# Turned probabilities in the weights' raw buffers, a tick between rotation and split, and earlier loads of queries and keys

## The chip, the cores and the metric

The kernel runs on one core of a Trainium2 chip. The core has a matrix engine (TensorE, PE in the profile, with its weight loads as PEld), a vector engine (VectorE, DVE), a scalar engine (ScalarE, ACT), a general engine (GpSimd, POOL) and a queue engine (SyncE, SP) that here only issues DMAs. The engines run side by side, each in the order of its own instructions, and wait for each other by semaphores. The metric is the device time of one execution in microseconds (us).

## What is computed

Two layers (DEPTH = 2) over 512 positions of width 2048. One projection of the layer's input is cut into three groups of heads, each 128 wide; every group is gated, all are joined, projected back, added to the input and normalised.

```python
    fq, fk, fv, fg, f_logit, dq, dk, dv, dg, iq, ik, iw, mq, mg = jnp.split(h, offsets, axis=-1)
    y_fox = fox_attention(heads(fq, H_FOX), ..., cum_logf) * silu(fg)           # 6 heads, causal, log-forget bias
    y_dsa = dsa_attention(rope(dq), rope(dk), dv, q_idx, k_idx, w_idx) * silu(dg) # 6 heads, rotated, top-128 keys
    y_mem = memory_attention(mq, k_mem, v_mem) * silu(mg)                        # 4 heads on 256 memory rows
    y = jnp.einsum('bsn,nd->bsd', jnp.concatenate([y_fox, y_dsa, y_mem], axis=-1), w_out)
    x = layer_norm(ALPHA * x + y, ln_gain, ln_bias)
```

The sparse heads (`d`) pick 128 keys per query by an index score; in the kernel that choice is a mask which is added to the scores. The forgetting heads (`f`) add a bias that falls with distance. Everything is float32.

## The kernel before

**Precision and tiling.** Each float32 operand is split in two float32r parts: ScalarE copies the high part, VectorE subtracts to get the low part (`split`, lines 216 to 218). A product is three matmuls, high x high, high x low, low x high (`product`, lines 224 to 226). Weights come in chunks of 128 x 2048; a chunk is two halves of 128 x 1024, and the main loop does one half per step: step n = 2i + h is half h of chunk i.

**Stages of a layer.** Memory keys and values, an index stage, the value stage (`vs` chunks: seven products in place of eight, for all columns that are handled in blocks), the heads stage (eight chunks `fq`, `fk`, `dq`, `dk` of heads 4 and 5, with the attention of eleven heads and one memory head between their matmuls), and the output stage (`out` chunks). A step takes 24 matmuls of 512 columns in the heads stage and 12 in the value and output stages.

**Weights.** `load_w(i + 2)` at the first step of chunk i issues both halves of chunk i + 2 on SyncE's queue (line 263), into two of the seven raw buffers of the pool `raws` (4 KB per partition each). `split_w(n + 3)` in step n splits half n + 3 into one of four pairs of `whl`. A raw buffer is free again when VectorE has made the low part. Some chunks are no loads at all: they are grown from a raw buffer that is kept (`grow_w`, `make_w`); of some others (`pair`) both halves of two blocks are loaded and added.

**Everything else** lies in 69 slots of 128 x 512 (2 KB per partition), among them the 32 of the layer's input, which stay. A slot or a raw buffer that the program asks for is one whose last use lies earlier in the program's order; the first instruction on it waits for that use to be over. SyncE issues in order, so a load that waits for its slot holds up all loads behind it.

**Order of the head work.** It is written out as generators: each `yield 1` ends a piece, and `tick` runs one piece of each active generator. The heads stage has two ticks per step, one in the middle of the chunk's matmuls and one behind them, 32 in all. `begin(gen, wait)` puts a generator in the list, and it sits out `wait` ticks first.
- `head_turn(l, v)` is called once per step, v = 0 to 15. It loads the queries and keys of the head that `TURNS` has at v + 2 (`load_qk`, two loads by line 998), begins `qk_head` of the head at v + 1, and begins `attend` of the head at v.
- `qk_head` turns the queries by PE transposes (line 1005), rotates them if the head is a sparse one (`rope`, lines 589 to 592: four VectorE operations, one of full height by the cosines, two of half height by the sines, one sum), splits them, ends its piece, and does the same for the keys.
- `attend` has five pieces: scores, masked minimum (line 763), exponentials (line 767), and the load of the gates; the load of the values; ten transposes of the probabilities in three PSUM tiles (line 788) and their split; the gates (`tanh`, line 507) and the split of the values; the product with the values (`po`) and the multiplication by the gates. The probabilities are divided by their sums (lines 771 and 774) at the next break in the chunk's matmuls.
- The turned probabilities are two tiles of 512 columns and one of 256: slots `pth` and `ptl` for each of the first two, one slot `pthl` for both parts of the third. They live from the third piece to the fifth.

`PRODUCTS` order, `OUT_ORDER` and the sums of weights that GpSimd's queue makes in DRAM (line 417) run beside all this and are paced by the ticks.

Of the kernel before, what the change touches and what calls it, by code (L numbers as in the profile page):

```python
# [11 lines left out]
F32 = mybir.dt.float32  # L12
F32R = mybir.dt.float32r
# [4 lines left out]
P = 128  # L18
DM = 2048
# [30 lines left out]
EARLY = 4  # L50
# [33 lines left out]
PAIRS = 6  # L84
# [92 lines left out]
def kernel(  # L177
# [13 lines left out]
    nc = tc.nc  # L191
# [11 lines left out]
    def uid(name):  # L203
        count[0] += 1
        return f"{name}_{count[0]}"

    def slot(name, dt=F32, w=512):
        return slots.tile([P, w], dt, tag="s", name=uid(name))
# [20 lines left out]
    chunks = stream()  # L229
# [14 lines left out]
    H = DM // 2  # L244

    def half(src, h):
        return src[:, h * H:(h + 1) * H]

    def load_w(i, pieces=2):
        if i < len(chunks) and chunks[i][4][0] != "grown":  # L250
            kind, key = chunks[i][4]
            src = {"wall": lambda: wall[key], "sum": lambda: sums[key],
                   "pair": lambda: wall[key[0]]}[kind]()
            if chunks[i][0] == "out" and chunks[i][2][0] == "Q6":
                raw[i] = [[slot("grown") for _ in range(2)] for _ in range(2)]
                for c in range(4):
                    nc.sync.dma_start(raw[i][c // 2][c % 2], src[:, c * 512:(c + 1) * 512])
                return
            raw[i], w = [], DM // pieces
            for c in range(pieces):  # L260
                if c * 2 % pieces == 0:
                    raw[i].append(raws.tile([P, H], F32, tag="raw", name=uid("raw")))
                nc.sync.dma_start(raw[i][-1][:, c * w % H:c * w % H + w], src[:, c * w:(c + 1) * w])
                if i < 3 and c * 2 % pieces == 0:
                    load_mem(2 * i + c * 2 // pieces)
                if kind == "pair":
                    for e in (2 * c, 2 * c + 1):
                        t = slot("other")
                        nc.sync.dma_start(t, wall[key[1]][:, e * 512:(e + 1) * 512])
                        others[i, e] = t  # L270
# [207 lines left out]
    def begin(gen, wait=0, last=False, whole=False, but=None):  # L478


        active.append([wait, gen, last, whole, but])
# [105 lines left out]
    def rope(ps, cos, sin, pairs, rows, name):  # L587
        t1, t2 = slot(name), slot(name)
        nc.vector.tensor_tensor(t1[:rows], ps[:rows], cos[:rows], op=ALU.mult)
        for a, b, n in pairs:  # L590
            nc.vector.tensor_tensor(t2[a:a + n], ps[b:b + n], sin[b:b + n], op=ALU.mult)  # L591
        nc.vector.tensor_tensor(t1[:rows], t1[:rows], t2[:rows], op=ALU.add)
        return t1
# [150 lines left out]
    def attend(l, kind, h):  # L744
        key = (kind, h)
        if kind == "f":
            bt = pr = biases.pop(h)
        q, k = qs.pop(key), ks.pop(key)
        ps = [bank("s") for _ in range(3)]
        for qb in (3, 1, 0, 2):  # L750
            b, off, w = PACK[qb]
            product(ps[b][:, off:off + w], tuple(a[:, qb * P:(qb + 1) * P] for a in q),
                    tuple(a[:, :w] for a in k), True, True)
        if kind == "d":
            assert l in chosen
            bt = masks[l]
            pr = [slot("pr", w=w) for w in BANK_W]
        nm, sums, rec = small("nm", 4), small("sums", 4), small("rec", 4)

        for qb in (3, 1, 0, 2):  # L760
            b, off, w = PACK[qb]
            c = slice(off, off + w)
            nc.vector.tensor_tensor_reduce(pr[b][:, c], ps[b][:, c], bt[b][:, c], -SCALE, -TAKEN,  # L763
                                           ALU.add, ALU.min, nm[:, qb:qb + 1])
        for qb in (3, 1, 0, 2):
            b, off, w = PACK[qb]
            nc.scalar.activation(pr[b][:, off:off + w], pr[b][:, off:off + w], AF.Exp,
                                 bias=nm[:, qb:qb + 1], scale=-1.0, accum_out=sums[:, qb:qb + 1])

        def probabilities():  # L770
            nc.vector.reciprocal(rec, sums)
            for qb in (3, 1, 0, 2):
                b, off, w = PACK[qb]
                nc.scalar.activation(pr[b][:, off:off + w], pr[b][:, off:off + w], AF.Copy,
                                     scale=rec[:, qb:qb + 1])

        before.append(probabilities)
        n = HEADS.index(key)
        load_head(("g", key), GATES + n // 4, n % 4)
        yield 1  # L780
        load_head(("v", key), VALUES + n // 4, n % 4)
        yield 1
        tp = [bank("pt") for _ in range(3)]
        for kt in range(4):
            tb, toff = PT_PACK[kt]
            for qb in range(kt, 4):
                b, off, w = PACK[qb]
                nc.tensor.transpose(tp[tb][:, toff + (qb - kt) * P:toff + (qb - kt + 1) * P],
                                    pr[b][:, off + kt * P:off + (kt + 1) * P], ident)
        pt = []  # L790
        for b in range(3):
            w = PT_W[b]
            if w == 512:
                hi, lo = slot("pth", F32R), slot("ptl", F32R)
            else:
                both = slot("pthl", F32R)
                hi, lo = both[:, :w], both[:, w:]
            split(tp[b][:, :w], hi, lo)
            pt.append((hi, lo))
        yield 1  # L800
        gate(key, turned(("g", key), "gt"))
        v = slot("vh", F32R), slot("vl", F32R)
        split(vraw.pop(("v", key)), *v)
        yield 1
        po = bank("po")
        for kt in range(4):
            tb, toff = PT_PACK[kt]
            w = SEQ - kt * P
            product(po[:, kt * P:], tuple(a[:, kt * P:(kt + 1) * P] for a in v),
                    tuple(a[:, toff:toff + w] for a in pt[tb]), kt == 0, kt == 3)  # L810
        heads_out(head_number(key), key, po)
# [196 lines left out]
    def load_qk(key):  # L1008
        for e in range(2):
            load_head(("qk"[e], key), (FOXQ if key[0] == "f" else DSAQ) + e, key[1])  # L1010

    def qk_head(key):
        for name, to in (("q", qs), ("k", ks)):
            t = turned((name, key), "qk")
            if key[0] == "d":
                t = rope(t, cos_d, sin_d, HALVES, P, "rope")
            hi, lo = slot("qh", F32R), slot("ql", F32R)
            split(t, hi, lo)
            to[key] = (hi, lo)
            yield 1  # L1020

    def head_turn(l, v):

        if v + 2 in TURNS and TURNS[v + 2][1] < EARLY:
            load_qk(TURNS[v + 2])
        if v + 1 in TURNS and TURNS[v + 1][1] < EARLY:
            key = TURNS[v + 1]
            begin(qk_head(key), 1)
            if key[0] == "f":
                load_ck(l, key[1])  # L1030
                begin(forget_bias(l, key[1]), 1)
        if v in TURNS:
            begin(attend(l, *TURNS[v]), 1 + (v in (11, 15)), whole=True)
        if v in MEM_TURNS:
            begin(mem_head(l, MEM_TURNS[v]), whole=True)
        if v in (8, 10, 12, 14):
            first_difference(v // 2 - 4)
        if v == 14:
            begin(early_operands())
# [159 lines left out]
    for i, (kind, l, j, col, _) in enumerate(chunks):  # L1199
# [28 lines left out]
        for h in range(2):  # L1228
            n = 2 * i + h
            grow_w(n + 2)  # L1230
            if h == 0 and i > 0:
                load_w(i + 2)
                if 2 <= i < 6:
                    for k in range(4 * i - 8, 4 * i - 4):
                        load_xt(k)
                elif i == 7:
                    load_tables()
# [134 lines left out]
            begin(top_keys(l), whole=True)  # L1372
        if kind == "vs" and (name, pair, col) == ("Q6", 0, 1) and l > 0:
            begin(residual_rows(l), whole=True)
        if kind == "vs" and (name, col) == ("Q3", 1):
            if pair in (1, 3, 5):
                begin(mem_head(l, pair // 2), whole=True)
            if pair == PAIRS - 3:
                load_ck(l, 0)
                load_qk(("f", 0))  # L1380
            elif pair == PAIRS - 2:
                begin(qk_head(("f", 0)), 5)
                begin(forget_bias(l, 0), 2)
            elif pair == PAIRS - 1:
                load_ck(l, 4)
                load_qk(("f", 1))
                begin(attend(l, "f", 0), 1, whole=True)
        if kind == "vs" and (name, pair, col) == ("Q3", PAIRS - 1, 1):
            chains.clear()
# [104 lines left out]
```

## Time and profile before

| what | us |
|---|---|
| median of three runs (1976.32 to 1979.19) | 1978.86 |
| the profiled execution, its own time | 1978.29 |
| its span | 1976.5 |
| heads stage of layer 0, by PE's timeline | about 615 to 820 |
| heads stage of layer 1 | about 1600 to 1803 |
| DMA, share of the 16 engines in layer 0's heads stage | 0.91 |

A window's row holds its length, the busy time of each engine with its number of instructions in brackets, the clock that TensorE was granted (1.00 is full), the mean share of the 16 DMA engines, and GB/s. A row of waits holds who waited, by engine, tile and line, behind the arrow what ended the wait, then the total in us, how often, and the longest. SPq is SyncE's queue; a row of its timeline has start, duration until the last of the group was issued, and the number of DMAs.

### The profile page before, as it was taken

To read this page: it belongs to the slowest core of one execution; us is meant where nothing else is said; L and a number is where in the kernel's file an instruction comes from. 1 tells how busy PE (TensorE), PEld (TensorE's weight loads), DVE (VectorE), ACT (ScalarE), POOL (GpSimd) and SP (SyncE) were. 2 spreads that over 40 slices of the span, in tenths; PEclk is the share of its full clock that TensorE was granted. 3 is DMA by queue.
4 is the path that set the end of the run, shared out by engine and by line. 5 is a ranking of instruction groups with operands and counts; after the bars stand their busy time and mean duration, and the time that the engine had idled before them with its cause. 6 is when DMAs were issued, how large, how long until landed. Compare 5 with 4: busy or idle time off the path is not lost.

```text
span 1976.5 us, 26877 instructions
## 1 busy us (share of the span) xinstructions
PE 1904.0 (96%) x9218; PEld 1611.5 (82%) x9218; DVE 1538.6 (78%) x2478; ACT 1061.0 (54%) x1674; POOL 408.6 (21%) x650
## 2 busy tenths in 40 slices
PE   9999999999999889899999999999999998788997
PEld 8998888888888777787899988888888886677876
DVE  6889777889666666888897898888886657578798
ACT  5775444445456654654476754444455565556553
POOL 0122112111113122131062211111211221211311
PEclk9999999999999999999999999999999999999999
DMA  9888889989999989899889867777899998886975
GB/s 352 291 235 224 255 242 274 276 246 279 314 321 300 267 223 263 286 290 310 263 259 280 233 202 203 234 225 214 229 305 313 333 282 244 236 229 207 269 215 140
DMA packets 190004, 511.95 MB, mean 259 GB/s; under 512 B 18656, under 2 KB 71904, under 8 KB 182124
## 3 DMA queue, kind: packets, MB, share of 16 engines
q1 hardware_dynamic: 146508, 303.63, 44.8%
q0 software_dynamic: 43360, 206.62, 42.0%
q8 instruction: 72, 1.18, 0.2%
q14 instruction: 64, 0.52, 0.1%
HBM read 456.67 MB, written 164.65 MB: 314 GB/s over the span
## 4 chain that ended last, share of the span: by engine, by line
PE 78%; DVE 8%; DMA 7%; ACT 4%; issue 2%; SPq 0%; POOL 0%; DVEq 0%; ACTq 0%; POOLq 0%
PE v L226 16%; PE v L224 16%; PE v L225 16%; PE c L226 5%; PE c L224 5%; PE c L225 5%; DMA raw<-in_wall_dram 4%; PE z L225 3%; PE z L226 3%; PE z L224 3%; DMA grown<-in_wall_dram 2%; DVE rope L591 1%; DVE wlo L218 1%; PE ix L704 1%; PE ix L705 1%
## 5 line engine op out<-in xcount | busy, mean ns | idle before, releaser
L218 DVE TENSOR_TENSOR wlo<-raw,whi 128x1024 fp32r<-128x1024 f32 (+1 forms) x513 | 628.4, 1231 | 244.1 <-ACT whi L217 238.6
L217 ACT ACTIVATE whi<-raw 128x1024 fp32r<-128x1024 f32 (+1 forms) x513 | 540.0, 1057 | 461.1 <-PE v L226 310.7
L224 PE MATMUL v<-whi,vxh 128*128 128x512 f32 x768 | 300.3, 391 | 1.0 <-ACT vraw L979 1.0
L226 PE MATMUL v<-whi,vxl 128*128 128x512 f32 x768 | 299.1, 389 | 0.0
L225 PE MATMUL v<-wlo,vxh 128*128 128x512 f32 x768 | 298.9, 389 | 0.0
L224 PE MATMUL v<-whi,xh 128*128 128x512 f32 x576 | 224.2, 389 | 0.0
L226 PE MATMUL v<-whi,xl 128*128 128x512 f32 x576 | 224.1, 389 | 0.0
L225 PE MATMUL v<-wlo,xh 128*128 128x512 f32 x576 | 224.1, 389 | 0.0
L224 PE MATMUL c<-xh,whi 128*128 128x512 f32 (+1 forms) x544 | 203.7, 374 | 0.2 <-DVE nm L763 0.2
L226 PE MATMUL c<-xh,wlo 128*128 128x512 f32 (+1 forms) x544 | 200.2, 368 | 0.0
L225 PE MATMUL c<-xl,whi 128*128 128x512 f32 (+1 forms) x544 | 199.6, 367 | 0.0
L225 PE MATMUL z<-wlo,yh 128*128 128x512 f32 (+1 forms) x434 | 168.8, 389 | 4.2 <-DVE wlo L218 4.2
L224 PEld LDWEIGHTS v<-whi,vxh 128*128 128x128 f32 x768 | 144.2, 188 | 31.4 <-ACT vraw L979 1.8
L226 PEld LDWEIGHTS v<-whi,vxl 128*128 128x128 f32 x768 | 144.2, 188 | 30.1
L224 PE MATMUL z<-whi,yh 128*128 128x512 f32 (+1 forms) x434 | 168.4, 388 | 0.0
L225 PEld LDWEIGHTS v<-wlo,vxh 128*128 128x128 f32 x768 | 144.2, 188 | 29.7 <-DVE wlo L218 0.2
L226 PE MATMUL z<-whi,yl 128*128 128x512 f32 (+1 forms) x434 | 167.8, 387 | 0.0
L225 PEld LDWEIGHTS v<-wlo,xh 128*128 128x128 f32 x576 | 108.1, 188 | 22.7
L224 PEld LDWEIGHTS v<-whi,xh 128*128 128x128 f32 x576 | 108.1, 188 | 22.5
L226 PEld LDWEIGHTS v<-whi,xl 128*128 128x128 f32 x576 | 108.1, 188 | 22.4
L408 POOL TENSOR_TENSOR seen<-mark,mhalf 128x1 f32<-128x1 f32 x87 | 26.7, 307 | 479.0 <-DVE mark L407 449.6
L224 PEld LDWEIGHTS c<-xh,whi 128*128 128x128 f32 x544 | 103.8, 191 | 11.4 <-DVE nm L763 0.7
(232 smaller groups left out, 3449.1 us busy)
## 6 DMA issues: line engine op xcount, KB each, us to landing
raw<-in_wall_dram SPq DMA_DIRECT2D x330, 512.0 KB, 7.2
sum<-in_wall_dram POOLq DMA_DIRECT2D x52, 1024.0 KB, 11.3
raw<-sum SPq DMA_DIRECT2D x88, 512.0 KB, 7.8
v<-vraw POOLq DMA_DIRECT2D x144, 256.0 KB, 6.6
raw<-in_wall_dram POOLq DMA_DIRECT2D x56, 512.0 KB, 7.5
vraw<-v SPq DMA_DIRECT2D x96, 256.0 KB, 7.4
other<-in_wall_dram SPq DMA_DIRECT2D x80, 256.0 KB, 9.1
grown<-sum SPq DMA_DIRECT2D x32, 256.0 KB, 6.5
```

Source lines behind the costliest of these rows:

```text
L217: nc.scalar.activation(hi, src, AF.Copy)
L218: nc.vector.tensor_tensor(lo, src, hi.bitcast(F32), op=ALU.subtract)
L224: nc.tensor.matmul(ps, ah, bh, start=start, stop=False, skip_group_check=more)
L225: nc.tensor.matmul(ps, ah, bl, start=False, stop=False, skip_group_check=more)
L226: nc.tensor.matmul(ps, al, bh, start=False, stop=stop, skip_group_check=more)
L408: nc.gpsimd.tensor_tensor(seen, mark, mhalf, op=ALU.mult)
L591: nc.vector.tensor_tensor(t2[a:a + n], ps[b:b + n], sin[b:b + n], op=ALU.mult)
L704: nc.tensor.matmul(o, st[:, qb * P:(qb + 1) * P], kh2[:, :w], start=True, stop=False)
L705: nc.tensor.matmul(o, st[:, qb * P:(qb + 1) * P], kl2[:, :w], start=False, stop=True)
```

## The change

1. `attend` puts the two tiles of 512 columns in raw buffers, high part in the left half and low part in the right: two raw buffers in place of four slots per head. The third tile stays in its slot.
2. `load_w` can load one half (`some`). For chunks i > 8 whose chunk i + 2 is no `pair`, the first half is loaded at the first step of chunk i and the second half at its second step, in place of both at the first.
3. `qk_head` of a sparse head has three pieces: rotation of the queries; their split, and the rotation of the keys; the split of the keys. A forgetting head's two pieces stay.
4. `attend` of every sparse head in `TURNS` begins with a wait of 2. Before, only those at v = 11 and 15 did, the others with 1.
5. Queries and keys are loaded at v + 3 in place of v + 2, and those of `f` 1 behind product Q5 of the last pair of value columns in place of Q3.

```diff
-    def load_w(i, pieces=2):
+    def load_w(i, pieces=2, some=(0, 1)):
...
-                raw[i] = [[slot("grown") for _ in range(2)] for _ in range(2)]
-                for c in range(4):
-                    nc.sync.dma_start(raw[i][c // 2][c % 2], src[:, c * 512:(c + 1) * 512])
+                for h in some:
+                    t = [slot("grown") for _ in range(2)]
+                    raw.setdefault(i, []).append(t)
+                    for c in range(2):
+                        nc.sync.dma_start(t[c], half(src, h)[:, c * 512:(c + 1) * 512])
...
             for c in range(pieces):
+                if c * 2 // pieces not in some:
+                    continue
...
-            if w == 512:
-                hi, lo = slot("pth", F32R), slot("ptl", F32R)
-            else:
-                both = slot("pthl", F32R)
-                hi, lo = both[:, :w], both[:, w:]
+            both = raws.tile([P, H], F32R, tag="raw", name=uid("pthl")) if w == 512 else slot("pthl", F32R)
+            hi, lo = both[:, :w], both[:, w:]
...
             if key[0] == "d":
                 t = rope(t, cos_d, sin_d, HALVES, P, "rope")
+                yield 1
             hi, lo = slot("qh", F32R), slot("ql", F32R)
             split(t, hi, lo)
             to[key] = (hi, lo)
-            yield 1
+            if key[0] == "f" and name == "q":
+                yield 1
+        yield 1
...
-        if v + 2 in TURNS and TURNS[v + 2][1] < EARLY:
-            load_qk(TURNS[v + 2])
+        if v + 3 in TURNS and TURNS[v + 3][1] < EARLY:
+            load_qk(TURNS[v + 3])
...
-            begin(attend(l, *TURNS[v]), 1 + (v in (11, 15)), whole=True)
+            begin(attend(l, *TURNS[v]), 1 + (TURNS[v][0] == "d"), whole=True)
...
             grow_w(n + 2)
+            if i > 0:
+                late_half = i > 8 and i + 2 < len(chunks) and chunks[i + 2][4][0] != "pair"
+                if late_half:
+                    load_w(i + 2, 2, (h,))
+                elif h == 0:
+                    load_w(i + 2)
             if h == 0 and i > 0:
-                load_w(i + 2)
...
+        if kind == "vs" and (name, pair, col) == ("Q5", PAIRS - 1, 1):
+            load_qk(("f", 1))
...
-                load_qk(("f", 1))
```

More of the change, by code (lines that the diff above doesn't have):

```diff
@@ L254, in load_w @@
             if chunks[i][0] == "out" and chunks[i][2][0] == "Q6":
-                raw[i] = [[slot("grown") for _ in range(2)] for _ in range(2)]
-                for c in range(4):
-                    nc.sync.dma_start(raw[i][c // 2][c % 2], src[:, c * 512:(c + 1) * 512])
+                for h in some:
[3 more added lines that the diff above has]
+                        nc.sync.dma_start(t[c], half(src, h)[:, c * 512:(c + 1) * 512])
                 return
-            raw[i], w = [], DM // pieces
+            w = DM // pieces
             for c in range(pieces):
+                if c * 2 // pieces not in some:
+                    continue
                 if c * 2 % pieces == 0:
-                    raw[i].append(raws.tile([P, H], F32, tag="raw", name=uid("raw")))
+                    raw.setdefault(i, []).append(raws.tile([P, H], F32, tag="raw", name=uid("raw")))
                 nc.sync.dma_start(raw[i][-1][:, c * w % H:c * w % H + w], src[:, c * w:(c + 1) * w])
```

## The prediction

> **What bounds the kernel now.** First the head of the page: TensorE is busy nearly all of the span, so what can be won is its idle time and its throttled time. All sums are made against the profiled execution, 1978.29 us (span 1976.5 and 1.8 around it); the median of the runs is 1978.86, 0.6 above, and I leave that out.
>
> ```profile
> span 1976.5 us, 26877 instructions
> PE 1904.0 (96%) x9218; PEld 1611.5 (82%) x9218; DVE 1538.6 (78%) x2478; ACT 1061.0 (54%) x1674; POOL 408.6 (21%) x650
> ```
>
> Second, the view by windows, cut at the stages: value stage and heads stage of layer 0, the same heads stage in layer 1, the end, and nine microseconds inside a heads stage.
>
> ```profile
> 150.00:550.00 400.00, 400.00 (x1779) 331.68 (x1778) 322.26 (x453) 194.58 (x227) 77.21 (x109) 1.00 0.92 265
> 615.00:820.00 205.00, 179.98 (x933) 150.66 (x932) 139.32 (x317) 113.02 (x261) 44.40 (x102) 0.93 0.91 260
> 1600.00:1803.00 203.00, 173.60 (x914) 144.99 (x913) 136.45 (x309) 110.91 (x257) 43.11 (x97) 0.94 0.85 238
> 1805.00:1976.00 171.00, 159.34 (x736) 131.46 (x734) 143.19 (x231) 82.72 (x126) 33.74 (x45) 0.98 0.73 211
> 756.00:765.00 9.00, 7.00 (x32) 5.84 (x31) 4.87 (x10) 5.32 (x10) 2.06 (x4) 0.81 0.83 165
> ```
>
> In the value stage PE is busy 400.00 of 400 at full clock: nothing to win there, only to lose. The two heads stages hold 25.0 and 29.4 us of idle PE, 54.4 of the 72.5 us that PE is idle in the whole span, and they run at a clock of 0.93 and 0.94: 14.4 and 12.2 us more at most. Part of the slow time is itself idle, so I count two thirds of these 26.6 as loss, 18 us. The pot is about 72 us.
>
> Third, who ends PE's waits in the heads stages (layer 0, then layer 1).
>
> ```profile
> PE gt L1005 <- DVE rec L771: 6.0, 1, 6.0
> PE s L224 <- ACT qh L217: 5.1, 2, 3.7
> PE po L224 <- ACT vh L217: 4.2, 3, 1.9
> PE ptm L573 <- ACT pm L565: 3.3, 1, 3.3
> PE pt L788 <- DVE ptl L218: 1.7, 1, 1.7
> PE s L224 <- DVE ptl L218: 1.4, 1, 1.4
> PE gt L1005 <- DMA vraw<-v: 1.3, 1, 1.3
> ```
>
> ```profile
> PE po L224 <- ACT vh L217: 11.4, 4, 7.3
> PE s L224 <- ACT qh L217: 5.0, 2, 3.7
> PE ptm L573 <- ACT pm L565: 4.9, 1, 4.9
> PE gt L1005 <- DVE ptl L218: 2.5, 1, 2.5
> PE pt L788 <- DVE ptl L218: 2.1, 1, 2.1
> PE s L224 <- DVE ptl L218: 1.4, 1, 1.4
> ```
>
> All but one are waits for ScalarE or VectorE, and both are only 55% and 68% busy there. So it is not their throughput: they sit in order behind something. The next rows say behind what: ScalarE's waits on the rotation (both layers) and on weights, and VectorE's wait in the group of splits that follow a rotation.
>
> ```profile
> ACT qh L217 <- DVE rope L592: 31.1, 11, 4.8
> ACT qh L217 <- DVE rope L592: 30.9, 11, 4.7
> ACT whi L217 <- DMA raw<-in_wall_dram: 1.7, 1, 1.7
> ACT whi L217 <- DMA raw<-in_wall_dram: 6.5, 1, 6.5
> L218 DVE TENSOR_TENSOR ql<-rope,qh 128x512 fp32r<-128x512 f32 x11 | 7.6, 693 | 7.9 <-ACT qh L217 7.9
> L591 DVE TENSOR_TENSOR rope<-qk,tabs 64x512 f32<-64x512 f32 x16 | 11.0, 688 | 0.2
> ```
>
> Each rotation of four VectorE operations (about 2.8 us) has its split right behind it: ScalarE stands 2.8 us per split (31.1 / 11), with exponentials and weight splits queued behind, and then VectorE stands 0.72 us for ScalarE (7.9 / 11). Eight of the eleven are queries and keys of heads 0 to 3 (sixteen half-height products, two each); the other three belong to the chunks of heads 4 and 5, whose code is not touched.
>
> Last, SyncE's queue, which issues the weights. Its waits, three pieces of its timeline, and the time from issue to landing of the weights in layer 0's heads stage:
>
> ```profile
> SPq L998 <- PE po L226: 32.3, 8, 9.4
> SPq L998 <- PE qk L1005: 27.6, 5, 9.1
> SPq L998 <- PE s L226: 25.9, 5, 11.4
> SPq L998 <- DVE ql L218: 16.5, 2, 11.2
> ```
>
> ```profile
> 711.47 3.44 SPq L263 DMA_DIRECT2D raw<-in_wall_dram  x2
> 717.98 24.05 SPq L998 DMA_DIRECT2D vraw<-v  x4
> 742.09 1.41 SPq L263 DMA_DIRECT2D raw<-in_wall_dram  x2
> ```
>
> ```profile
> DMA to landing us min/median/max: 5.1/12.7/26.4
> ```
>
> SyncE waits over 100 of 205 us in line 998 (a head's queries, keys, values or gates) for a slot that a matmul or a split has yet to release, and never notably in line 263 (a weight into a raw buffer). So slots are what is short, raw buffers are not, and weights stand behind slots. That made one half late per layer: 1.7 us and 6.5 us of ScalarE, which show up in the 6.0 (gt) and the 7.3 (po) above.
>
> **The change part by part.**
>
> *Turned probabilities in raw buffers.* No instruction is added: the same split writes elsewhere. Per head, four slots go and two of the seven raw buffers come, from the split to the head's product, two ticks. Eleven heads over 32 ticks: 11 x 4 x 2 / 32 = 2.75 slots fewer on average. Fetching queries and keys one step (two ticks) sooner takes back 7 heads x 2 x 2 / 32 = 0.9. Net, SyncE gets slots somewhat sooner. I take it that the two late halves come on time: 1.7 off the gt wait, 6.5 off the po waits. Ends: nothing, and 1.7 + 6.5 twice if exponentials that stood behind them also move PE a second time (16 us).
>
> The new wait: a split on ScalarE, or a weight on SyncE, may now wait for a raw buffer. ScalarE's split comes after the earlier splits in its own order, so it waits at most for VectorE's half of a pair, 0.69 us. Behind SyncE's wait stand all later loads. In code order, one or two weight halves and two raw buffers of probabilities are alive (four for one tick, where heads d4 and f3 are one tick apart), so at most six of seven. Nothing below zero: I see no way in which this wait saves time.
>
> *Second halves a step later.* No DMA is added, only its place: behind the loads that the first step's ticks issue. In the value and output stages a step is 2.7 us, and SyncE there waits for raw buffers anyway:
>
> ```profile
> SPq L263 <- DVE raw L302: 159.8, 19, 21.7
> ```
>
> (19 waits within 150 to 400 us.) Order within a queue that is held by buffers costs nothing; cover is PE's 400.00 of 400. In the output stage PE is idle 11.7 of 171, tail included, and I allow 0 to 3 us. In the heads stage a step is 12.8 us (205 / 16), and the half is split one step later in code order: slack 12.8 against a median landing of 12.7. That is the change's price, and no row shows it. Ends: nothing (SyncE runs a step ahead), and the rival below. I put 12 us for this and for any wait on raw buffers, nearest to the rows of the late halves: two stalls like layer 1's 6.5.
>
> *Rotation and split in different ticks, and four of the six sparse heads in the turns (d0, d1, d2, d3) start a tick later.* A tick is about 6.4 us (205 / 32), more than any wait on a rotation (4.8). ScalarE's 8 x 2.8 = 22 us per layer of standing go, and VectorE's 8 x 0.72 = 5.8. On the path I take, both layers together:
> - s after qh, 10.1: gone; the scores come a tick later (6.4 us) than their longest wait (3.7).
> - ptm after pm, 8.2: one round trip shorter, 0.75 wait + 0.69 split, and the first sparse head's exponentials go a tick back: 2 stay.
> - the five waits on ptl, 9.1: each loses up to 1.4 us: 3 stay.
> - gt after rec, 6.0: minus 1.4 and the 1.7 of the late half: 3 stay.
> - po after vh, 15.6: minus 6.5 for the late half and 1.1: 8 stay.
> - the rest, 5.4 (54.4 less the five sums): stays.
>
> Removed: 10.1 + 6.2 + 6.1 + 3.0 + 7.6 = 33 of 54.4. Ends: only the two sums that hang directly on the late half and the split (10.1 + 8.2 = 18), and all 49 listed. Of the clock's 18 us the same share, 0.6, goes: 11.
>
> **Sum:** 33 + 11 - 12 = 32. 1978.3 - 32 = **1946**.
>
> On the clock: where stalls fall from 6 to 3 us, does the slow phase go with them? The row 756 to 765 has a clock of 0.81 though the longest stall in it is one of the 1.9 us kind, so small stalls bring it too, and I let it shrink only in proportion. [...]
>
> **The rivals.**
> - *Slots stay short.* 1.9 slots on average may not carry SyncE past its waits of up to 11.4 us. Then the 8.2 of the late halves and a third of the clock's gain (3) are not won: 1957. For: the waits are many. Against: four slots are about a fifth of the twenty that one head's code takes in turn.
> - *The slow phases vanish wholly,* because short stalls between dense matmuls no longer add up: 7 more: 1939. The row of 0.81 speaks against it.
> - *Stalls only move.* VectorE's work is unchanged (139 of 205), a later head collides with the next, and raw-buffer waits eat the rest: 1977, no change.
> - *Slower: second halves land late.* 16 of them (8 chunks, 2 layers) have 12.8 us if SyncE reaches them no sooner than in code order. Half land later than 12.7, by about (26.4 - 12.7) / 2 = 6.9 us: 8 x 6.9 = 55 against the 44 gained: 1989. It decides at the point where SyncE issues line 263 less than some 13 us before ScalarE's split. For: the 24.05 us in which SyncE stood before 742.09. Against: that stand was itself lengthened by PE's 6.0 us stall and by the slots that are now freed.
>
> **How the numbers follow.** Forecast 0.48 (its own range 1930 to 1965), slots short 0.16, clock 0.12, stalls move 0.09, slower 0.15. Faster by over 0.2% (4 us, about what a measurement of this kernel tells from no change): 0.48 + 0.16 + 0.12 = 0.76; within: 0.09; slower: 0.15. The range takes in the first four, the unknown costs' ends and the start of the slower case: 1925 to 1980; about 0.05 lies below and 0.11 above.
>
> **What would show it.** ScalarE's wait on the rotation falls from 31.1 and 30.9 us to a third (the chunks' own rotations); PE's s after qh disappears; SyncE's line 998 waits less; PE's idle in the heads windows falls from 54.4 to about 30, its clock rises to about 0.96. Wrong would be: SyncE waiting in line 263 for a product of probabilities, ScalarE waiting for weights in many places, or idle PE in the value windows.

## The result, and the profile after

The changed kernel takes 1957.24 us (median of four runs, 1951.81 to 1959.12), the kernel before 1979.03 (median of four): ratio 0.9873, 95% interval 0.9828 to 0.9919. The forecast was 1946 and the range 1925 to 1980. Faster was right and the time lies in the range, but the gain is 22 us where 32 were forecast. A second series on another occasion (e9 below) gave 0.9903 (0.9878 to 0.9928).

The head of the page of the changed kernel (busy time of each engine, share of the span, instructions):

```profile
span 1957.4 us, 26870 instructions
PE 1896.9 (97%) x9218; PEld 1609.8 (82%) x9218; DVE 1532.5 (78%) x2478; ACT 1058.4 (54%) x1674; POOL 408.7 (21%) x650
```

The same work in a shorter span: PE is idle 60.5 us where it was 72.5. The next view cuts the changed kernel at its two heads stages, which I take from PE's timeline (from the first matmul into the chunks' tile `c` to the first one of the output stage); the two short windows are explained at the end.

```profile
617.00:810.00 193.00, 173.51 (x919) 145.96 (x917) 133.33 (x310) 110.66 (x257) 44.46 (x102) 0.96 0.96 272
1596.00:1784.00 188.00, 169.41 (x917) 143.19 (x915) 132.89 (x304) 110.39 (x257) 45.48 (x100) 0.97 0.91 256
741.00:748.00 7.00, 5.24 (x22) 4.16 (x22) 6.21 (x11) 3.50 (x6) 0.70 (x2) 0.80 1.13 376
786.00:793.00 7.00, 4.99 (x22) 4.01 (x22) 6.18 (x11) 4.96 (x10) 0.65 (x2) 0.76 1.15 369
```

By the same cut, stage for stage in the profiled executions:

| stage | before, us | after, us | difference |
|---|---|---|---|
| heads, layer 0 | 202.9 | 193.1 | -9.8 |
| heads, layer 1 | 204.8 | 188.2 | -16.6 |
| value stage, layer 1 | 471.1 | 475.2 | +4.1 |
| memory and index stage, layer 1 | 143.9 | 145.7 | +1.8 |
| output stage, layer 0 | 163.5 | 165.1 | +1.6 |
| all other stages | 790.3 | 790.1 | -0.2 |

So the heads stages won 26.4 us, and 7.5 were given back elsewhere. The place of the 7.5 is not fixed: in a second trace of the changed kernel (e9) the value stage of layer 1 takes 471.7 us and the output stage of layer 0 takes 168.2. The 4.1 us of the value stage here are mostly one stall of PE, which ends at 1557.5 us after 3.2 us, and the slow clock behind it (0.50 from 1557.6 to 1561.0 us); the prediction had named idle PE in this stage as a sign of being wrong. Within the heads stages PE's idle time went from 54 to 38 us (193 less 173.5, and 188 less 169.4), and the clock rose to 0.96 and 0.97, as forecast. Who ends PE's waits there now (engine, tile, line, releaser: total, times, longest; the change moves line 788 to 792 and 774 to 778), layer 0 and layer 1:

```profile
PE pt L792 <- ACT pr L778: 4.8, 2, 3.8
PE pt L792 <- ACT bt L778: 2.7, 1, 2.7
PE po L224 <- ACT vh L217: 2.4, 2, 1.5
...
PE s L224 <- ACT qh L217: 1.6, 2, 1.3
```

```profile
PE pt L792 <- ACT pr L778: 5.6, 2, 5.1
PE po L224 <- ACT vh L217: 5.3, 3, 3.3
PE po L226 <- DVE vl L218: 3.2, 2, 2.8
```

The scores hardly wait any more for the split of queries (10.1 us in both layers before, 1.6 now); the memory head's transposes wait for nothing. In their place stands a wait that was 1.5 us before: the transposes of probabilities wait for ScalarE to divide them, 13 us in both layers. The longest of these waits can be followed back in layer 1:

```profile
1666.13 0.69 DVE L596 TENSOR_TENSOR rope<-rope,rope 128x512 f32<-128x512 f32 x1
1667.47 0.73 ACT L771 ACTIVATE pr<-pr,nm 128x512 f32<-128x512 f32 x1 [5.17 <-DVE nm L767]
1673.61 2.48 PE L792 MATMUL pt<-ident,pr 128*128 128x128 f32 x10 [5.13 <-ACT pr L778]
```

VectorE takes the masked minimum of this head (line 767) only behind other pieces in its order, the last of them the rotation of another head's rows. So ScalarE stands 5.17 us for the minimum, the exponentials and the division come late, and PE stands 5.13 us.

ScalarE's own waits on the rotation and on weights, and SyncE's in the weights' line (267 now), first layer 0, then layer 1:

```profile
ACT qh L217 <- DVE rope L596: 12.3, 6, 3.0
ACT whi L217 <- DMA raw<-in_wall_dram: 7.2, 1, 7.2
SPq L267 <- PE po L226: 12.2, 3, 6.1
```

```profile
ACT qh L217 <- DVE rope L596: 13.1, 7, 2.9
SPq L267 <- PE po L226: 14.3, 3, 8.0
```

ScalarE's standing behind rotations fell from 31 us per layer to 12 or 13, close to the third that was forecast. SyncE's waits in the line of head loads (998, now 999) fell as well, from 144 to 107 us in layer 0 and from 157 to 112 in layer 1. But one late weight half is there still, in layer 0 now, and SyncE waits with weights for products of probabilities: the sign that the prediction named for the raw buffers going wrong.

### The profile page after: what moved, and what is told of

It reads as the page before. It is cut to its first block, busy times and chain, and to the rows that moved or that the text cites. A ratio compares the mean times of both kernels' runs of the same rounds, so it can differ in the third digit from the quotient of the medians.

```text
span 1957.4 us, 26870 instructions
## 1 busy us (share of the span) xinstructions
PE 1896.9 (97%) x9218; PEld 1609.8 (82%) x9218; DVE 1532.5 (78%) x2478; ACT 1058.4 (54%) x1674; POOL 408.7 (21%) x650
## 4 chain that ended last, share of the span: by engine, by line
PE 80%; DVE 8%; DMA 5%; ACT 4%; issue 2%; POOL 1%; SPq 0%; DVEq 0%; ACTq 0%; POOLq 0%
PE v L224 16%; PE v L226 16%; PE v L225 16%; PE c L226 5%; PE c L224 5%; PE c L225 5%; PE z L225 4%; PE z L226 4%; PE z L224 4%; DMA raw<-in_wall_dram 2%; DVE rope L595 1%; DVE wlo L218 1%; DMA grown<-in_wall_dram 1%; DMA grown<-sum 1%; PE ix L708 1%
## 5 line engine op out<-in xcount | busy, mean ns | idle before, releaser
L226 PEld LDWEIGHTS c<-xh,wlo 128*128 128x128 f32 x544 | 102.6, 189 | 12.1
```

The lines of the kernel that those rows point to most:

```text
L226: nc.tensor.matmul(ps, al, bh, start=False, stop=stop, skip_group_check=more)
```

## Experiments

The parts of the change can be taken one by one. Part 1 is the raw buffers, 2 the second halves a step later, 3 the pieces of the rotation, 4 the later start, 5 the sooner queries and keys. Ratios are to the kernel before on the same chip, with 95% intervals.

**e1: parts 3 and 4 alone.**

```diff
                 t = rope(t, cos_d, sin_d, HALVES, P, "rope")
+                yield 1
...
-            begin(attend(l, *TURNS[v]), 1 + (v in (11, 15)), whole=True)
+            begin(attend(l, *TURNS[v]), 1 + (TURNS[v][0] == "d"), whole=True)
```

> Only the rotation and the split in pieces of their own, and the later start of the sparse heads' attention; turned probabilities in slots, both halves loaded together, queries and keys at v + 2. Theory A (the in-order round trip between VectorE and ScalarE was most of the stall): idle PE in the two heads windows falls from 54.4 to about 35, the time by 15 to 20 us, ratio 0.990 to 0.993; ScalarE's wait on the rotation falls to a third. Theory B (slots were what was short, the rest only followed): under 6 us, ratio 0.997 or more, SyncE's line 998 waits as before.

1965.13 us, ratio 0.9925 (0.9903 to 0.9947): theory A's time, and its third of the wait on the rotation, but not its idle PE, of which 46 us are left in the two heads stages in place of 35. ScalarE's waits in layer 1's heads stage, however, hold this:

```profile
ACT whi L217 <- DMA raw<-in_wall_dram: 11.0, 2, 6.5
ACT qh L217 <- DVE rope L592: 10.3, 6, 3.1
```

The rotation's wait is down to a third, and late weights are worse than before (6.5): the heads run faster (199 us in place of 204.8), and the weights do not come sooner.

**e2: parts 1 and 2 alone.**

```diff
+            both = raws.tile([P, H], F32R, tag="raw", name=uid("pthl")) if w == 512 else slot("pthl", F32R)
...
+                if late_half:
+                    load_w(i + 2, 2, (h,))
```

> Only the turned probabilities in raw buffers and the second halves a step later. Theory A: the late weight halves come on time, 8 us of stall and 3 of clock less in the heads stages, 7 more outside them from second halves that stand behind other loads: ratio 0.996 to 1.000. Theory B: most of the gain of 22 us is here: ratio 0.988 to 0.992.

1986.79 us, ratio 1.0036 (1.002 to 1.0053): slower, outside what both theories had. PE's waits over the whole of it:

```profile
PE po L224 <- ACT vh L217: 13.1, 7, 7.0
PE s L224 <- ACT qh L217: 9.7, 4, 3.7
PE ptm L577 <- ACT pm L569: 8.7, 2, 5.4
```

They are the waits of before. Free slots alone removed none of them. The late half of layer 1 is gone in this trace, but one of 7.5 us has come up in layer 0's heads stage, where it was 1.7. Theory B fell here, and theory A's small gain did not come either.

**e3: all but part 2** (both halves at the first step).

```diff
-            if i > 0:
-                late_half = i > 8 and i + 2 < len(chunks) and chunks[i + 2][4][0] != "pair"
-                if late_half:
-                    load_w(i + 2, 2, (h,))
-                elif h == 0:
-                    load_w(i + 2)
             if h == 0 and i > 0:
+                load_w(i + 2)
...
```

> The whole change, but both halves of a chunk loaded at its first step, as before. If the later second halves cost the 7 us by which the stages outside the heads stage got longer (value stage of layer 1 by 4.1, index and output stages by 1.6 and 1.8), this is about 1950 us, ratio 0.985 or less, with no throttled phase at the end of layer 1's value stage. Rival: the raw buffers are then too few (up to three weight halves and four of probabilities alive), SyncE waits in the weights' line for products of probabilities, and the heads stages lose 5 us or more: ratio 0.990 or more.

1958.63 us, ratio 0.9885 (0.9856 to 0.9915): no better than the whole change. Its four times are 1948.03, for the profiled execution, and 1958.30 to 1960.48 for the three others, so its trace shows an execution that is not the usual one. In it ScalarE waits for no weights in the heads stages, the value stage of layer 1 is 471.8 us, as before, and SyncE waits in the weights' line for products, 16.1 us in layer 0. Inconclusive: the trace looks as if the later halves cost something, the times say that leaving them out gains nothing, and e9's trace has 471.7 us in that value stage with the later halves in place.

**e4: all but part 5** (queries and keys at v + 2, those of `f` 1 behind Q3).

```diff
-        if v + 3 in TURNS and TURNS[v + 3][1] < EARLY:
-            load_qk(TURNS[v + 3])
+        if v + 2 in TURNS and TURNS[v + 2][1] < EARLY:
+            load_qk(TURNS[v + 2])
...
```

> The whole change, but queries and keys loaded at v + 2, as before. If the sooner fetch matters little (PE waits for a DMA of a head's rows only 1.3 to 2.3 us in all, before and after), ratio 0.986 to 0.990. If it is what makes the new pieces possible (rows must be there a step sooner because the rotation is spread), PE or VectorE waits for these loads and the ratio is 0.993 or more.

1965.06 us, ratio 0.993 (0.9907 to 0.9953): like e1. The prediction had put nothing on the sooner fetch; by the medians it carries about a third of the gain (7 to 8 of 22 us), though the interval touches that of the whole change. Without it the raw buffers add nothing to the steps. What waits is not what the expectation named: ScalarE waits for weights, 9.9 and 10.8 us in the two heads stages, where the changed kernel has 7.2 and nothing.

**e5: all but parts 1 and 2,** that is, parts 3, 4 and 5 with the probabilities in slots.

> Steps of their own, later start and sooner queries and keys, but turned probabilities in slots and both halves loaded together. If the raw buffers' part is to pay for the sooner fetch (their four slots per head are what the early rows then occupy), the sooner fetch wins nothing here: like the steps alone, ratio 0.992 to 0.996, and SyncE's line of head loads waits over 90 us in layer 0's heads window. If the sooner fetch works without them, ratio 0.987 to 0.990, and moving the probabilities was for nothing.

1951.44 us, ratio 0.9864 (0.9848 to 0.9881). The sooner fetch finds its slots without the raw buffers, and beside e1 it brings 12 to 14 us, with intervals that do not overlap. To tell this kernel from the whole change, both ran again beside each other in five rounds.

**e9: the changed kernel again.**

> The changed kernel itself, beside e10 on the same chip, so that the two can be told apart. Theory C (the raw buffers and late second halves win nothing and cost a little): about 1957 us, 3 to 8 us above e10. Rival: the two are equal within 2 us.

**e10: e5 again.**

> Steps of their own, later start, sooner queries and keys; probabilities in slots, both halves together. Theory C: 1950 to 1954 us, ratio 0.985 to 0.988, below e9.

e9: 1958.48 us, ratio 0.9903 (0.9878 to 0.9928). e10: 1947.35 us, ratio 0.9846 (0.9825 to 0.9868). The intervals do not overlap: parts 1 and 2 together cost 11 us here, where the change gains 19 and e10 gains 30. (Between e5 and the first series of the changed kernel, which ran on other occasions, it is 6 us and the intervals overlap.) e10 is the fastest kernel of the study. Its windows of the two heads stages:

```profile
617.00:807.00 190.00, 170.52 (x917) 143.78 (x916) 133.41 (x310) 110.60 (x257) 44.69 (x102) 0.96 0.97 277
1585.00:1773.00 188.00, 167.74 (x923) 142.88 (x922) 133.14 (x305) 110.91 (x257) 44.57 (x98) 0.98 0.94 266
```

Its heads stages hardly differ from the changed kernel's (190 and 188 us beside 193 and 188). The rest of the difference between these two traces lies in the output stage of layer 0 (163.5 us beside 168.2 in e9's trace) and in a microsecond here and there (memory and index stage 143.9 beside 145.1). In the first trace of the changed kernel this output stage took 165.1, so which part of parts 1 and 2 costs what, and where, stays open.

**e6: all but part 3** (rotation and split in one piece, later start kept).

```diff
                 t = rope(t, cos_d, sin_d, HALVES, P, "rope")
-                yield 1
...
```

> The whole change, but rotation and split in one piece as before; the later start of the sparse heads stays. Theory: of the gain of the steps (15 us alone), the in-order round trip of rotation and split is the larger part: ratio 0.992 to 0.996, ScalarE waits about 31 us per layer on the rotation again, s after qh stays small because the start is later. Rival: the later start alone does it, by spreading the heads: 0.987 to 0.990 although ScalarE's waits on the rotation are back.

1964.31 us, ratio 0.993 (0.9908 to 0.9953). ScalarE's wait on the rotation is back, in layer 1's heads stage:

```profile
ACT qh L217 <- DVE rope L596: 28.2, 11, 4.4
```

By the medians the pieces are worth 6 to 7 us; the interval touches that of the whole change, so the size is uncertain.

**e7: all but part 4** (pieces kept, start as before).

```diff
-            begin(attend(l, *TURNS[v]), 1 + (TURNS[v][0] == "d"), whole=True)
+            begin(attend(l, *TURNS[v]), 1 + (v in (11, 15)), whole=True)
```

> The whole change, but the sparse heads' attention starts as early as before: scores then come in the same tick as the split of the keys. Theory: PE's wait s after qh or ql is back (up to 10 us in the two layers), ratio 0.990 to 0.994. Rival: the pieces alone suffice, 0.986 to 0.989.

1976.72 us, ratio 0.9987 (0.9971 to 1.0002): nothing of the gain is left, worse than the theory had. PE's two longest waits, whole span:

```profile
PE s L224 <- ACT qh L217: 19.9, 6, 4.5
PE s L225 <- DVE ql L218: 10.7, 8, 2.7
```

With the split of the keys a tick later, scores that start as early as before stand at once behind it, 31 us. The later start is what the pieces need; it is worth 18 to 20 us beside the rest. It is also what brings the new wait: transposes of probabilities wait for the division 2.7 us in this kernel, which has the pieces without the later start, and 17.4 us in e6, which has the later start without the pieces.

**e8: the changed kernel with 65 slots.**

```diff
-    slots = ctx.enter_context(tc.tile_pool(name="slots", bufs=69))
+    slots = ctx.enter_context(tc.tile_pool(name="slots", bufs=65))
```

> The changed kernel with 65 slots in place of 69. If freed slots carry part of the gain, four fewer take back what the raw buffers gave (7 to 10 us): ratio 0.990 to 0.995, SyncE's waits for slots grow. If there are now slots to spare, 0.986 to 0.989.

1984.78 us, ratio 1.0037 (1.0013 to 1.006): worse than the kernel before. Four slots are worth 26 to 28 us by the medians; the ten executions scatter widely (1978.55 to 1997.08), and the profiled one, 1978.74, is among the fastest. They are worth it not in the heads stages alone: between 1000 and 1600 us ScalarE waits for weights 32.9 us, in the changed kernel 23.1. So slots are short indeed, yet e10, which holds four more per head, is faster. Either what the raw buffers free is not what the loads lack, or it costs as much in raw buffers; no run tells these apart.

**e11 and e12: why the sooner fetch gains.** By then the theory was that order matters: at v + 2 two heads' loads stand ahead of one chunk's weights and none ahead of the next, at v + 3 one head's ahead of each. e11 (on e1) has one head's pair ahead of each chunk's weights, with half of the heads sooner; e12 (on e1) has all sooner, and two by two again.

```diff
-        if v + 2 in TURNS and TURNS[v + 2][1] < EARLY:
-            load_qk(TURNS[v + 2])
+        for t in (v + 2, v + 3):
+            if v % 2 and t in TURNS and TURNS[t][1] < EARLY:
+                load_qk(TURNS[t])
```

> As e1 (steps and later start alone), but queries and keys of the heads with an even turn are loaded one step sooner, those with an odd turn as before: one head's pair of loads ahead of each chunk's weights in SyncE's queue, in place of two heads' ahead of one and none ahead of the next. Theory D (the sooner fetch wins because it takes half of these loads out of the way of the weights): 1948 to 1955 us, ratio 0.984 to 0.989, ScalarE waits for weights under 2 us in the heads stages. Theory E (what counts is that the rows are there sooner): half of e5's extra gain at most, 1957 to 1962 us, ratio 0.989 to 0.991.

```diff
-        if v + 2 in TURNS and TURNS[v + 2][1] < EARLY:
-            load_qk(TURNS[v + 2])
+        if v + 4 in TURNS and TURNS[v + 4][1] < EARLY:
+            load_qk(TURNS[v + 4])
```

> As e1, but queries and keys of all heads two steps sooner (v + 4): sooner than in the change, yet again two heads' loads between the same two chunks' weights. Theory D: no better than e1, 1960 us or more, ratio 0.990 or more, ScalarE waits for weights. Theory E: as good as e5 or better, ratio 0.988 or less. A third way: the early rows hold slots two steps longer, and SyncE waits for slots so long that it is slower than e1.

e11: 1959.75 us, 0.9906 (0.9882 to 0.9931). e12: 1949.13 us, 0.9868 (0.983 to 0.9907). Both medians lie where theory E has them, though each interval still touches theory D's range. ScalarE's wait for weights in layer 1's heads stage speaks against D more clearly; e11 was to have under 2 us of it:

```profile
ACT whi L217 <- DMA raw<-in_wall_dram: 13.4, 3, 6.0
```

In e12, where D expected such waits, and in e5 and e10, this row does not occur in either heads stage. So the even spacing of D is not what counts. The same pair of weights, issued by SyncE and its first half split by ScalarE, in e1 and then in e5:

```profile
1684.07 1.04 SPq L263 DMA_DIRECT2D raw<-in_wall_dram  x2
...
1705.04 1.06 ACT L217 ACTIVATE whi<-raw 128x1024 fp32r<-128x1024 f32 x1 [4.51 <-DMA raw<-in_wall_dram]
```

```profile
1673.72 1.81 SPq L263 DMA_DIRECT2D raw<-in_wall_dram  x2
...
1690.36 1.05 ACT L217 ACTIVATE whi<-raw 128x1024 fp32r<-128x1024 f32 x1
```

In e1 ScalarE wanted it 16.5 us after the issue (1705.04 less the wait of 4.51, less 1684.07), in e5 16.6 us after: the pair is not issued earlier against its use, it lands sooner. Of the pair's two halves, from issue to landing, first e1, then e11, e5 and e12:

```profile
DMA to landing us min/median/max: 20.9/21.6/22.3
DMA to landing us min/median/max: 22.0/22.5/23.1
DMA to landing us min/median/max: 15.2/17.8/20.3
DMA to landing us min/median/max: 10.4/13.3/16.2
```

SyncE's queue shows one difference directly ahead of the pair, in the same order of kernels:

```profile
1681.88 1.59 SPq L998 DMA_DIRECT2D vraw<-v  x3
1678.38 1.56 SPq L998 DMA_DIRECT2D vraw<-v  x3
1672.55 0.36 SPq L998 DMA_DIRECT2D vraw<-v  x1
1676.74 0.36 SPq L998 DMA_DIRECT2D vraw<-v  x1
```

In e1 and e11 three loads of heads are issued in the 2.2 us ahead of these weights, two of them the queries and keys of `d` 2; in e5 and e12 it is one load, because those two were issued a step or two earlier. e11 loads all its queries and keys at odd v, the last step ahead of a chunk's weights, so it does not separate "sooner" from "not directly ahead of the weights". That head loads in flight hold back the weights behind them is therefore the likely cause, with the DMA engines at least 0.9 busy in 29 of 40 equal slices of the time from 1684 to 1705 us in e1, and in 25 of 40 from 1673.7 to 1690 us in e5; no run isolates it.

## Why the prediction was right, and where it was off

- **Stalls by the rotation: right.** s after qh was to go (10.1 us): 1.6 is left. ScalarE's wait on the rotation was to fall to a third of 31 us: 12 and 13. ptm after pm: gone. e1 alone brings 15 us. e7 shows that the later start, by which the prediction let the largest of these sums go, is the part without which the rest is nothing.
- **The late halves: wrong.** "I take it that the two late halves come on time" rested on the free slots. e2 has the free slots and a half that is 7.5 us late; the changed kernel has one of 7.2. What took late weights away, in e5, e10 and e12, was the sooner fetch, which the prediction counted only as a cost in slots (0.9 of them) and to which it gave no gain. Without the raw buffers it brings 12 us or more (e5 and e10 beside e1).
- **The price of raw buffers and later halves: right in size, in part by luck.** 12 us were put down, and 11 measured (e9 against e10). The 12 stood for two late weight halves in the heads stages; of the 11, the traces of e9 and e10 show some 2 us there and 5 in the output stage of layer 0. How much of it is the wait for raw buffers, which the trace shows (12 and 14 us of SyncE's time), and how much the later halves, e3 does not settle.
- **PE's idle time in the heads stages: a term mis-sized.** 33 of 54 us were to go; 16 did. The five sums on the list did fall, from 49 to 13 us, a little more than forecast. But the rest, 5.4 us, which was to stay, became 25, and 13 of these are the transposes that wait for the division. "The rest stays" was the wrong step. e6 and e7 show that the later start makes the new wait; in the code the pieces of a head keep their distances, so what changed is which other work stands ahead of them in the engines' order. e10, without parts 1 and 2, has 40 us of idle PE in its heads stages too, so this shortfall is not the price of the raw buffers.
- **Rival "stalls only move": half there.** "A later head collides with the next" is what the new wait of 5.13 us shows. It took back about 20 of the 36 us, not all of them.
- **Clock: right in size, not in its rule.** 11 us were put down, and PE's busy time in the heads windows, for nearly the same matmuls, fell by 10.7 (179.98 and 173.60 before, 173.51 and 169.41 after). But the loss was to shrink in proportion to the idle time. Idle time fell by 0.3, and the loss (length of the window times what the clock lacks to 1.00) by half, from 26.6 to 13.4 us. The rival with no slow phases fell.
- **Slower rival:** its mechanism is there (weights waiting for products, a half that is late), at a fifth of its price at most (11 of 55 us).

Added up in the prediction's terms, 16 us of idle time and 10 of clock were won in the heads stages and 7.5 were lost elsewhere: 19 us between these two executions, 22 by the medians, 32 by forecast. The total missed by less than its largest term (17 us), in part because less was lost elsewhere than the 12 us put down; that is luck, not insight.

## What to carry to other kernels

Where engines wait though none is full, look for two instructions on two engines that stand directly behind each other in both orders, and put a piece of other work between them; then move what consumes them by the same piece, or the stall only changes its place, as in e7 (31 us). Before freeing a resource because a queue waits for it, take a little of it away and give a little of it alone: the waits on slots were the longest in SyncE's list, four slots fewer cost 26 us, and still the exchange of slots for raw buffers lost. And try each part by itself: the parts that help gain 30 us here, and the other two take 11 of them back.

## What was not expected of the hardware

The slow clock came behind stalls as short as 1.5 us. In the changed kernel's windows 741 to 748 and 786 to 793 us the granted clock is 0.80 and 0.76. PE's stalls at the first of them, and shortly ahead of it, are these two (the wait stands in brackets), with eight transposes and twelve matmuls of full width between them:

```profile
738.54 0.63 PE L1006 MATMUL gt<-ident,vraw 128*128 128x128 f32 x4 [1.56 <-DMA vraw<-v]
...
743.88 0.50 PE L224 MATMUL po<-pthl,vh 128*128 128x512 f32 x1 [1.51 <-ACT vh L217]
```

Behind the second one the clock is 0.50, from 745.21 us on. Between 600 and 1850 us this trace has nine slow phases at 0.50, eight of 3.41 us and one of 6.83. Cut into stretches of 3.41 us that join on to this one, the trace reads:

```profile
734.97:738.38 3.41, 2.01 (x9) 1.31 (x7) 2.94 (x10) 1.44 (x5) 0.00 (x0) 1.00 1.05 412
741.80:745.21 3.41, 1.65 (x7) 0.75 (x6) 2.71 (x6) 3.02 (x5) 0.70 (x2) 1.00 1.00 304
745.21:748.62 3.41, 3.41 (x17) 3.41 (x16) 3.35 (x6) 0.53 (x2) 0.00 (x0) 0.50 1.10 411
```

The first stretch, which holds most of the first stall, has PE idle for 1.40 us (3.41 less 2.01), and the clock stays at 1.00 behind it. The second has PE idle for 1.76 us, and the clock is 0.50 in the next. The traces of the kernel before and of the changed kernel, cut in the same way between 600 and 1850 us in step with their slow phases, agree. Of the stretches at a clock of 1.00, all 13 in which PE was idle for more than 0.6 of it were followed by the slow clock, and none of the 679 in which it was idle for less than 0.4; of the 14 in between, 6 were. (Behind one slow stretch in each trace the slow clock went on although PE was idle for only 0.25 and 0.32 of it.) So in 6 of these 14 cases about half of a stretch sufficed, at 745.21 us in stalls of 1.51 us and less. The prediction's proportion to all idle time is not what these stretches show.
